# Attention probabilities transposed by DMA as 16-bit halves, with the heads of branches A and B at new slots

## The chip, the cores and the metric

The kernel runs on one core of a Trainium2 chip. The metric is the device time of one execution in microseconds. TensorE is called PE below, its weight loads PEld, VectorE DVE, ScalarE ACT, GpSimd POOL, and the queue that issues most DMAs SP. Each engine works through its own list of instructions strictly in the order in which the program issued them.

## The reference

One layer of a decoder, sequence 512, width 2048. The normed input is multiplied by one wide matrix that yields the inputs of three token mixers; two of them matter here, each with 12 heads of 64 channels:

```python
# branch A: window of 128 keys, in blocks of 128 queries by 256 keys
p = jnp.exp(scores - m)
denom = jnp.sum(p, axis=-1, keepdims=True) + jnp.exp(sink - m)
out = jnp.einsum('bnkgqs,bnskd->bnqkgd', p / denom, vb)
# branch B: causal attention with forget gates
sc = jnp.einsum('bqhd,bshd->bhqs', qb, k) * scale + cqb[..., None] - c[:, :, None, :]
p = jax.nn.softmax(jnp.where(mask[None, None], sc, NEG), axis=-1)
return jnp.einsum('bhqs,bshd->bqhd', p, v)
```

Branch C is a small cross attention. Each branch's output is gated, projected to 2048, weighted, summed, and goes through a last projection. All values are float32.

## The kernel before, in words

Every float32 product on PE is made of reduced-precision float32 products: an operand is split into a high part (`hi`, a cast on ACT) and a low part (`lo`, a subtraction on DVE), and hi·hi, hi·lo and lo·hi are summed in PSUM.

The program is one long stream of such products (`Stream`, L226). A unit of the stream multiplies 256 rows of a weight matrix with the activations: 24 matmuls of 384 or 512 columns. When unit i begins, the weights of unit i+1 are split (`w_split`, L206: two casts on ACT at L212, two subtractions on DVE at L215, the latter issued a little later) and those of unit i+2 are fetched (`weights`, L191, on SP). The split weights have two buffers, so the casts can't start before unit i-1 is done.

The attention heads are woven into that stream by a clock: `tick` (L146) is called after every third matmul of the stream and adds 0.5. Work is put on an agenda for a clock value (`later`, L143) or stands in a `Chain` (L165), a list of steps with offsets from a base. So one unit of 24 matmuls is 4 of the clock, and the place of a step in every engine's list is set by two tables: the base of a head (`BASES_B`, `BASES_A`) and the offset of a step (`STEPS_B`, `STEPS_A`). Preparations for pairs of heads (`prep`, `prep_q`, `prep_k`: transposes of queries or keys on PE, then two or four scalings on ACT through `q_stack` and `k_stack`) have slots of their own.

Branch B has its heads 0 to 5 beside the products that make the second half of B's queries, keys and values, and 6 to 11 beside A's. Branch A's 12 heads run beside the products z, mem and qC. One head of B (`head_B`, L583) does this: `s1(i)`, for query blocks i = 0 to 3: score products on PE of 128 to 512 keys, a fused add and row minimum on DVE (L600), an exponential on ACT (L603), a reciprocal and scaling (`scaled`, L579; on DVE for B, on POOL for A). POOL makes the biases (`sb`, L609). Then `s2(g)` transposes the probabilities in blocks of 128x128 on PE (L625) into PSUM, and `split` (L555) casts them to hi on ACT (L556) and subtracts lo on DVE (L558). Last `s3`: eight matmuls with V (L635, tile `avB`), each pair taking hi first and lo second, and `pv_out`, which adds up the two halves of the result. A head of B has 10 blocks to transpose; a head of A (`head_A`, L652; L688, L691, L702) has 7.

At the end of a product its four PSUM banks are read out on ACT (L437 for queries and keys, followed by squares for the norms at L404). In the stage of `mem` the activations, too, are split on ACT (`mhl`, L895). In a late stage the kernel already transposes by DMA for a part of its output (`flip_dma`: L1465 makes the halves, L1469 sends them, L1478 joins them).

Of the kernel before, what the change touches and what calls it, by code (L numbers as in the profile page):

```python
# [12 lines left out]
F32 = mybir.dt.float32  # L13
# [21 lines left out]
BASES_B = ((14, 24, 35.5, 46, 52, 70.5), (15, 24, 34.5, 47, 58, 72.5))  # L35
BASES_A = (12.5, 17, 23.5, 37.5, 43, 48.5, 52, 70.5, 75.0, 79.5, 81, 89)
BASES_C = (12.0, 19.5, 28.0, 33.5)
STEPS_B = (-12, -8.5, -2, -1.5, 0, 1, 1.0, 1.5, 3.5, 5, 12, 11.5, 14, 15.5)
STEPS_A = (-5.0, -1.0, -0.5, -1.5, 6.5, 8, 11, -6.5)
STEPS_C = (-8, -3.5, 0.5, 1, 8.0, 4.5, 10)  # L40

PREP_Q = ((-1.5, 22.0, 38.5), (2.5, 18.5, 45.5))
PREP_K = ((6.5, 28.0, 44), (7, 26.5, 53.5))
PREP_A = (6, 18.5, 39.0, 46, 66.0, 76.5)
PREP_KA = (6.0, 32.5, 47.5, 68.0)
# [12 lines left out]
def tile_hybrid_block(ctx, tc, xT, x, memT, mem, ng, mng, w_in, b_forget, gqa, gka, sinks, gqb, gkb, gqc, gkc,  # L58
# [100 lines left out]
    free = {"T": 2, "P": 2, "PT": 1, "Q": 3, "KH": 3, "KL": 2, "bias": 2, "cb": 2}  # L159
# [230 lines left out]

    def qk_tile(name, tag, n, bufs):
        return tokp.tile([P, NT, n], F32, tag=tag, bufs=bufs, name=name)
# [30 lines left out]
    def evac_qk(key, tag, n, hd, bufs, scale=rstd, nt=NT, after=None):  # L423
# [4 lines left out]
        def f(b, pb, c0=0):  # L428
            if after is not None:
                after(b, pb)  # L430
            if b == 0:
                state["t"] = tokp.tile([P, nt, n], F32, tag=tag, bufs=bufs, name=f"t_{key}")
# [10 lines left out]
    def evac_v(key, nh):  # L443
        state = {}

        def f(b, pb, c0=0):
            if b == 0:
                state["v"] = tokp.tile([P, NT, nh, P], F32R, tag="V", bufs=1, name=f"V_{key}")
# [3 lines left out]
            ac.activation(v[:, b, :, 0:64], src, AF.Copy, scale=rstd[:, b:b + 1])  # L452
            ve.scalar_tensor_tensor(out=v[:, b, :, 64:128], in0=src, scalar=rstd[:, b:b + 1],
                                    in1=f32(v[:, b, :, 0:64]), op0=ALU.mult, op1=ALU.subtract)
# [128 lines left out]
    def head_B(h, kv):  # L583
# [3 lines left out]
        def s1(i):  # L587
# [16 lines left out]
            later(DIV_B, lambda: scaled(pi, den, i, ve))  # L604

# [8 lines left out]
        def s2(g):  # L614
            p = s["p"]
            if g == 0:
                s["hi"] = at.p.tile([P, 1280], F32R, tag="PH", bufs=1, name=f"phB{h}")
                s["lo"] = at.p.tile([P, 1280], F32R, tag="PL", bufs=1, name=f"plB{h}")
            off = (0, 128, 384, 768)
            grp, o, n = (((0,), 0, 512), ((1, 3), 512, 512), ((2,), 1024, 256))[g]  # L620
            tb = tbank(f"ptB{h}_{grp[0]}")
            c = 0
            for j in grp:
                for i in range(j, NT):
                    pe.transpose(tb[:, c:c + P], p[:, off[i] + j * P:off[i] + (j + 1) * P], ident)  # L625
                    c += P
            split(s["hi"][:, o:o + n], s["lo"][:, o:o + n], tb[:, :n])

        def s3():
            q, kh, kl, v, hv, cb = kv()  # L630
            av = avbank(f"avB{h}")
            for j in range(NT):
                n = S - j * P
                for w, t in enumerate((s["hi"], s["lo"])):
                    pe.matmul(av[:, j * P:], v[:, j, hv, :], t[:, BOFF[j]:BOFF[j] + n],  # L635
# [3 lines left out]
        def done():  # L639
# [5 lines left out]
                 (o[8], [], lambda: s1(2)), (o[9], [], lambda: (s1(3), done())),  # L645
                 (o[10], ["T", "PT"], lambda: s2(0)), (o[11], ["T"], lambda: s2(1)),
                 (o[12], ["T"], lambda: (s2(2), release("P"))), (o[13], ["T"], lambda: (s3(), release("PT")))]
# [4 lines left out]
    def head_A(h, kv):  # L652
# [27 lines left out]
        def s2(g):  # L680
            pv = s["p"]
            if g == 0:
                s["hi"] = at.p.tile([P, 1280], F32R, tag="PH", bufs=1, name=f"phA{h}")
                s["lo"] = at.p.tile([P, 1280], F32R, tag="PL", bufs=1, name=f"plA{h}")
            tb = tbank(f"ptA{h}_{g}")
            c = 0
            for j in (2 * g, 2 * g + 1):
                pe.transpose(tb[:, c:c + P], pv[:, j, 128:256], ident)  # L688
                c += P
                if j < NT - 1:  # L690
# [216 lines left out]
    def evac_m(b, pb):  # L907
# [10 lines left out]
        if t == 1:  # L918
            toks["mv"] = (v[:, 0], v[:, 1])
# [695 lines left out]
```

## Time and profile before

| | |
|---|---|
| median of 3 runs | 1481.18 us (1481.14 to 1482.17) |
| span of the profiled execution | 1480.7 us, 20354 instructions; the page gives no other time of it |
| PE busy | 1473.2 us, 99% |
| ACT busy | 727.5 us, 49% |
| heads of B, first half and second half | about 125 to 238 us and 250 to 360 us |
| heads of A | about 391 to 556 us |

The page is read from the top: busy time by engine, then the span in 40 slices, then the chain of work that ended last. PE is busy in every slice, so what keeps it busy or makes it wait sets the time; the other engines' idle time costs nothing unless PE waits for them.

### The profile page before, as it was taken

Reading aid. Unit: us, or ns where it says so; the run is one execution under the profiler, and the core shown is the slowest. Engines: PE = TensorE matmul, PEld = TensorE weight load, DVE = VectorE, ACT = ScalarE, POOL = GpSimd, SP = SyncE. Lnnn points to the kernel's source line nnn. Section 1 sums busy time; section 2 is a strip of 40 time slices with the busy share of each in tenths; the row PEclk is TensorE's granted clock in tenths of the full one; section 3 lists DMA queues with packets and bytes.
Section 4 is the critical chain, followed back from the end, with each engine's and each line's share of the span. In section 5 each row is a group of like instructions: output and inputs, shape, how many; then the busy total and the mean of one; then the engine's idle time right before and its main releaser. Section 6 shows DMA issues by size and latency. Waiting matters only on the chain.

```text
span 1480.7 us, 20354 instructions
## 1 busy us (share of the span) xinstructions
PE 1473.2 (99%) x7193; PEld 1272.6 (86%) x7193; DVE 1092.5 (74%) x1886; ACT 727.5 (49%) x1212; POOL 185.3 (13%) x223
## 2 busy tenths in 40 slices
PE   9999999999999999999999999999999999999998
PEld 9999999998888888888888888888888888888887
DVE  6385875775678666578888888888887566589997
ACT  5545654664467664555444443435354344245442
POOL 0121430331324430000000000000000201110000
PEclk9999999999999999999999999999999999999999
DMA  8774235333444323476667676767676876676674
GB/s 290 222 213 130 76 93 164 84 113 111 130 137 151 92 79 108 149 261 231 207 213 224 214 241 206 241 211 230 201 236 213 279 222 205 220 246 223 243 286 153
DMA packets 135630, 279.50 MB, mean 189 GB/s; under 512 B 22492, under 2 KB 62044, under 8 KB 135528
## 3 DMA queue, kind: packets, MB, share of 16 engines
q1 hardware_dynamic: 130488, 261.68, 55.8%
q10 hardware_dynamic: 5040, 16.53, 3.3%
q8 instruction: 56, 0.92, 0.2%
q14 instruction: 46, 0.38, 0.1%
HBM read 244.58 MB, written 31.48 MB: 186 GB/s over the span
## 4 chain that ended last, share of the span: by engine, by line
PE 96%; ACT 1%; DVE 1%; DMA 1%; issue 0%; POOL 0%; DVEq 0%; ACTq 0%; POOLq 0%
PE P L1085 41%; PE z L301 11%; PE qA L301 5%; PE kB L301 5%; PE vB L301 5%; PE uB L1085 4%; PE uA L1085 4%; PE qB L301 4%; PE qC L301 3%; PE kvA L301 3%; PE uC L1085 3%; PE mem L301 1%; PE avB L635 1%; PE ptB L625 1%; PE avA L702 1%; PE sB L577 1%
## 5 line engine op out<-in xcount | busy, mean ns | idle before, releaser
L215 DVE TENSOR_TENSOR wc<-wa,wb 128x512 fp32r<-128x512 f32 (+2 forms) x252 | 148.8, 629 | 75.3 <-ACT wb L212 71.7
L212 ACT CAST wb<-wa 128x512 fp32r<-128x512 f32 (+2 forms) x252 | 130.5, 567 | 146.3 <-PE z L301 34.5
L1127 ACT CAST wa<-rawl 128x1024 fp32r<-128x1024 f32 x85 | 89.4, 1052 | 208.1 <-DVE rawl L1017 149.8
L1017 DVE TENSOR_TENSOR rawl<-rawl 128x512 f32<-128x512 f32 x256 | 176.9, 692 | 6.3 <-DMA rawl<-in_w_out_dram 1.9
L1130 DVE TENSOR_TENSOR wc<-rawl,wa 128x1024 fp32r<-128x1024 f32 x85 | 105.0, 1235 | 52.0 <-ACT wa L1127 50.3
L1130 DVE TENSOR_TENSOR we<-rawl,wd 128x512 fp32r<-128x512 f32 (+1 forms) x128 | 122.2, 954 | 4.5 <-ACT wd L1127 0.9
L1401 POOL TENSOR_TENSOR y<-y,gA 128x512 f32<-128x512 f32 x16 | 28.1, 1788 | 727.8 <-DVE gA L1399 727.8
L1127 ACT CAST wd<-rawl 128x512 fp32r<-128x512 f32 (+1 forms) x128 | 106.9, 835 | 23.8 <-DVE rawl L1017 20.1
L301 PE MATMUL z<-ah,wb 128*128 128x512 f32 x256 | 101.8, 398 | 0.0
L301 PE MATMUL z<-ah,wc 128*128 128x512 f32 x256 | 99.9, 390 | 0.0
L301 PE MATMUL z<-al,wb 128*128 128x512 f32 x256 | 99.8, 390 | 0.0
L1127 ACT CAST wb<-rawl 128x1024 fp32r<-128x1024 f32 x43 | 45.3, 1053 | 87.4 <-DVE rawl L1017 62.1
L1085 PE MATMUL P<-wd,xhx 128*128 128x512 f32 x192 | 74.8, 390 | 0.0
L1085 PE MATMUL P<-we,xhx 128*128 128x512 f32 x192 | 74.7, 389 | 0.0
L1085 PE MATMUL P<-wd,xlx 128*128 128x512 f32 x192 | 74.7, 389 | 0.0
L1130 DVE TENSOR_TENSOR wb<-rawl,wb 128x1024 fp32r<-128x1024 f32 x43 | 52.5, 1222 | 25.5 <-ACT wb L1127 25.3
L1014 DVE TENSOR_TENSOR R<-P,R 128x512 f32<-128x512 f32 (+1 forms) x90 | 57.1, 674 | 6.4 <-PE P L1085 5.8
L301 PEld LDWEIGHTS z<-ah,wc 128*128 128x128 f32 x256 | 48.0, 188 | 10.2
L301 PEld LDWEIGHTS z<-ah,wb 128*128 128x128 f32 x256 | 48.1, 188 | 9.3 <-DVE zA L939 0.3
L301 PEld LDWEIGHTS z<-al,wb 128*128 128x128 f32 x256 | 48.2, 188 | 9.0
L581 POOL TENSOR_SCALAR pA<-pA,denA 128x256 f32<-128x256 f32 (+1 forms) x48 | 45.0, 953 | 79.5 <-DVE denA L580 79.5
L1085 PE MATMUL P<-wa,xlx 128*128 128x512 f32 x128 | 49.8, 389 | 0.0
(410 smaller groups left out, 4184.8 us busy)
## 6 DMA issues: line engine op xcount, KB each, us to landing
rawl<-in_w_in_dram SPq DMA_DIRECT2D x144, 512.0 KB, 4.5
rawl<-in_w_out_dram SPq DMA_DIRECT2D x48, 512.0 KB, 4.8
wa<-in_w_in_dram SPq DMA_DIRECT2D x62, 384.0 KB, 3.5
wa<-in_w_in_dram SPq DMA_DIRECT2D x64, 256.0 KB, 3.1
rawl<-in_w_in_dram SPq DMA_DIRECT2D x48, 256.0 KB, 4.1
gates<-R ACTq DMA_DIRECT2D x24, 512.0 KB, 7.3
wa<-in_w_in_dram SPq DMA_DIRECT2D x16, 512.0 KB, 3.7
wa<-in_w_mem_dram SPq DMA_DIRECT2D x16, 512.0 KB, 3.7
```

Of the source, the lines that this page charges most:

```text
L212: ac.copy(hi[:, :n], raw[:, i, :n])
L215: ve.tensor_sub(lo[:, :n], raw[:, i, :n], f32(hi[:, :n]))
L301: pe.matmul(pb, a, m, start=b in fresh, stop=last and not todo[b])
L577: pe.matmul(dst, q[:, qs], kl[:, ks], start=False, stop=True)
L581: engine.tensor_scalar(p, p, den[:, 4 + i:5 + i], None, op0=ALU.mult)
L625: pe.transpose(tb[:, c:c + P], p[:, off[i] + j * P:off[i] + (j + 1) * P], ident)
L1014: ve.tensor_tensor(out, a, b, op=ALU.add)
L1017: ve.tensor_tensor(out, a, b, op=ALU.subtract)
L1085: pe.matmul(*args, **kw)
L1127: ac.copy(hi[:, :k, :], src)
L1130: return lambda: ve.tensor_tensor(lo[:, :k, :], src, f32(hi[:, :k, :]), op=ALU.subtract)
L1401: po.tensor_tensor(y, y, g, op=ALU.add)
```

## The change

The 204 transposes of probabilities on PE go away (12 heads of B with 10, 12 of A with 7). In their place, for every head:

- `halves`: POOL copies the float32 probabilities, seen as pairs of 16-bit numbers, into a tile in which all first halves and all second halves lie apart (2560 numbers per partition for B in five copies, 1792 for A in three);
- `send`: one DMA transpose on SP, of 20 blocks of 128x128 16-bit numbers for B and 14 for A;
- `join`: one copy on ACT that puts the halves together again, into float32 in SBUF;
- `s2`: one cast on ACT to hi (1280 or 896 columns), and `s2l`: one subtraction on DVE to lo. Before there were three casts and three subtractions per head of B and two and two of A, each read from PSUM.

`head_A` gets the same functions with 896 columns; its `halves(True)` copies the first two query blocks, `halves(False)` the other two.

The new tiles take places freed by cutting V of branch B in two pieces (heads 0 to 3 and 4 to 5 of a half) and by reusing others. New names in `free` (S1, S2, RW) keep heads from overtaking each other there. All heads' bases, the preparations' slots and the offsets change.

```diff
-BASES_B = ((14, 24, 35.5, 46, 52, 70.5), (15, 24, 34.5, 47, 58, 72.5))
+BASES_B = ((14, 26, 38, 46, 58, 70), (14, 26, 38, 46, 58, 70))
-STEPS_B = (-12, -8.5, -2, -1.5, 0, 1, 1.0, 1.5, 3.5, 5, 12, 11.5, 14, 15.5)
+STEPS_B = (-12, -8.5, -2, -1.5, 0, 1, 1.0, 1.5, 3.5, 5, 10.5, 16.5, 18, 19, 20.5, 4.5)
-STEPS_A = (-5.0, -1.0, -0.5, -1.5, 6.5, 8, 11, -6.5)
+STEPS_A = (-5.0, -1.0, -0.5, -1.5, 6.5, 10.5, 11.5, -6.5, 3, 3.5, 12.5, 13.5)
...
+    def spare(n, name, dtype=F32, cols=1280):
+
+        return tokp.tile([P, 1280 * 4 // mybir.dt.size(dtype)], dtype, tag=f"X{n}", bufs=1, name=name)[:, :cols]
...
@@ evac_v
-            ac.activation(v[:, b, :, 0:64], src, AF.Copy, scale=rstd[:, b:b + 1])
+            for t, hs in zip(v, (slice(0, 4), slice(4, 6))):
+                ac.activation(t[:, b, :, 0:64], src[:, hs, :], AF.Copy, scale=rstd[:, b:b + 1])
...
@@ head_B
+            s["p", i] = pi
+            if i > 1:
+                later(DIV_B + 0.5, lambda: halves(i))
...
-            for j in grp:
-                for i in range(j, NT):
-                    pe.transpose(tb[:, c:c + P], p[:, off[i] + j * P:off[i] + (j + 1) * P], ident)
-                    c += P
-            split(s["hi"][:, o:o + n], s["lo"][:, o:o + n], tb[:, :n])
+        def halves(i):
+
+            if i == 0:
+                s["s1"] = spare(0, f"s1B{h}", U16, 2560).rearrange("p (e j n) -> p e j n", e=2, n=P)
+            src = u16(s["p", i]).rearrange("p (j n e) -> p e j n", n=P, e=2)
+            n = min(i + 1, 3)
+            po.tensor_copy(s["s1"][:, :, i:i + 3 * n - 2:3, :], src[:, :, :n, :])
+            if i == 3:
+                po.tensor_copy(s["s1"][:, :, 7:8, :], src[:, :, 3:4, :])
+                release("P")
+
+        def send():
+            s["s2"] = spare(1, f"s2B{h}", U16, 2560)
+            sy.dma_start_transpose(out=s["s2"].rearrange("p (x n) -> p x n", n=P),
+                                   in_=s["s1"].rearrange("p e j n -> p (e j n)"))
+            release("S1")
+
+        def join():
+            s["t"] = spare(2, f"ptB{h}")
+            ac.copy(u16(s["t"]).rearrange("p (n e) -> p e n", e=2), s["s2"].rearrange("p (e n) -> p e n", e=2))
+            release("S2")
+
+        def s2():
+            s["hi"] = at.p.tile([P, 1280], F32R, tag="PH", bufs=1, name=f"phB{h}")
+            s["lo"] = at.p.tile([P, 1280], F32R, tag="PL", bufs=1, name=f"plB{h}")
+            ac.copy(s["hi"], s["t"])
+
+        def s2l():
+            ve.tensor_tensor(s["lo"], s["t"], f32(s["hi"]), op=ALU.subtract)
+            release("RW")
...
-                 (o[10], ["T", "PT"], lambda: s2(0)), (o[11], ["T"], lambda: s2(1)),
-                 (o[12], ["T"], lambda: (s2(2), release("P"))), (o[13], ["T"], lambda: (s3(), release("PT")))]
+                 (o[10], ["S2"], send), (o[11], ["RW"], join), (o[12], ["PT"], s2), (o[13], [], s2l),
+                 (o[14], ["T"], lambda: (s3(), release("PT")))]
...
@@ head_A
-                (o[4], ["T", "PT"], lambda: s2(0)), (o[5], ["T"], lambda: (s2(1), release("P"))),
-                (o[6], ["T"], lambda: (s3(), release("PT")))]
+                (o[8], ["S1"], lambda: halves(True)), (o[9], [], lambda: halves(False)), (o[4], ["S2"], send),
+                (o[5], ["RW"], join), (o[6], ["PT"], s2), (o[10], [], s2l), (o[11], ["T"], lambda: (s3(), release("PT")))]
```

The tables move instructions on every engine; three places show how. The line numbers of the changed program are its own. First, ACT's list before, around head 1 of the first half of branch B: its three casts to `phB`, with the exponentials of the next head (`pB`, `denB`), the weight casts (`wb`, each x2 belongs to one unit), and the next pair's queries (`qB`).

```order
L556 CAST phB_1748<-ptB_0_1750 128x512
L556 CAST phB_1748<-ptB_1_1756 128x512
L212 CAST wb_1762<-wa_1694 128x384 x2
L603 ACTIVATE pB_1773,denB_1774<-pB_1773,denB_1774 128x128
L404 ACTIVATE sq_qB_1804<-t_qB_1625 128x384
L556 CAST phB_1748<-ptB_2_1806 128x256
L603 ACTIVATE pB_1773,denB_1774<-pB_1773,denB_1774 128x256
L212 CAST wb_1848<-wa_1766 128x384 x2
L566 COPY avsB_1859<-avB_1832 64x512
```

ACT's list now, for the same head: the copy from `s2B` to `ptB` is the join, and the cast to `phB` is `s2`.

```order
L212 CAST wb_1822<-wa_1754 128x384 x2
L616 ACTIVATE pB_1783,denB_1784<-pB_1783,denB_1784 128x384
L649 COPY ptB_1855<-s2B_1759 128x2x1280
L551 ACTIVATE qB_1878<-tqB_1873,gs_qb 64x512
L551 ACTIVATE qB_1880<-tqB_1873,gs_qb 64x512
L616 ACTIVATE pB_1783,denB_1784<-pB_1783,denB_1784 128x512
L655 CAST phB_1886<-ptB_1855 128x1280
L212 CAST wb_1894<-wa_1826 128x384 x2
L579 COPY avsB_1963<-avB_1938 64x512
```

The casts to hi were spread over three places, each behind its own transposes; now the join and one long cast stand between the last two exponentials of the next head and the weight casts of a unit, with the next pair's queries between them.

Second, DVE's list at the same place, before: the first two subtractions of `plB` of head 1, with the weight subtractions (`wc`), norms (`nr_qB`, `t_qB`) and the next head's first score block.

```order
L215 TENSOR_TENSOR wc_1691<-wa_1615,wb_1690 128x384 x2
L570 TENSOR_TENSOR ysB_1657<-avB_1648,avsB_1671 64x512
L415 TENSOR_TENSOR t_qB_1625<-t_qB_1625,nr_qB_1627 128x384
L558 TENSOR_TENSOR plB_1749<-ptB_0_1750,phB_1748 128x512
L558 TENSOR_TENSOR plB_1749<-ptB_1_1756,phB_1748 128x512
L600 ISA pB_1773,denB_1774<-sB_0_1775,biB_0_1723 128x128
```

DVE's list now: one subtraction of `plB`.

```order
L552 SCALAR_TENSOR_TENSOR qB_1878<-tqB_1873,gs_qb,qB_1878 64x512
L552 SCALAR_TENSOR_TENSOR qB_1880<-tqB_1873,gs_qb,qB_1880 64x512
L215 TENSOR_TENSOR wc_1895<-wa_1826,wb_1894 128x384 x2
L658 TENSOR_TENSOR plB_1887<-ptB_1855,phB_1886 128x1280
L593 RECIPROCAL denB_1784<-denB_1784 128x1
L594 TENSOR_SCALAR pB_1783<-pB_1783,denB_1784 128x512
```

`plB` now stands behind the subtractions `wc` that read the weights cast after `phB`, and ahead of the scaling of the next head's last block.

Third, ACT's list in the stage of `mem`, for head 3 of branch A, before (the casts to `phA` are its splits):

```order
L556 CAST phA_4926<-ptA_0_4928 128x512
L212 CAST wb_4934<-wa_4889 128x512 x2
L895 ACTIVATE mhl_4940<-mraw_4938,mngt 128x256 x2
L556 CAST phA_4926<-ptA_1_4958 128x384
L538 ACTIVATE qA_4981<-tqA_4976,gs_qa 64x512
```

and now:

```order
L212 CAST wb_4857<-wa_4839 128x512 x2
L739 COPY ptA_4870<-s2A_4797 128x2x896
L950 ACTIVATE mhl_4863<-mraw_4861,mngt 128x256 x2
L745 CAST phA_4893<-ptA_4870 128x896
L212 CAST wb_4901<-wa_4864 128x512 x2
L579 COPY avsA_4931<-avA_4919 64x512
```

The join comes right behind one unit's weight casts, and the cast to hi right ahead of the next unit's.

104 lines of the change are left out of this document (59 added, 45 removed).

## The prediction

> **What bounds the kernel now.** I read the page's head first, then what PE waited for, then the two attention stages (the first window is six heads of B, the second the twelve of A; columns: window, busy us and count of PE, PEld, DVE, ACT, POOL, then clock, DMA share, GB/s).
>
> ```profile
> span 1480.7 us, 20354 instructions
> ...
> PE 1473.2 (99%) x7193; PEld 1272.6 (86%) x7193; DVE 1092.5 (74%) x1886; ACT 727.5 (49%) x1212; POOL 185.3 (13%) x223
> ```
> ```profile
> PE warm_up L1540 <- DVE wz L1537: 1.9, 1, 1.9
> PE ptA L688 <- DVE kl L550: 0.7, 1, 0.7
> PE kB L301 <- ACT t_qB L437: 0.2, 1, 0.2
> ```
> ```profile
> 252.00:360.00 108.00, 108.00 (x610) 100.10 (x609) 77.34 (x203) 60.87 (x138) 33.96 (x52) 1.00 0.39 119
> 391.00:556.00 165.00, 164.22 (x867) 138.07 (x866) 116.60 (x310) 106.31 (x245) 63.06 (x67) 1.00 0.38 116
> ```
>
> PE is the bound everywhere, at full granted clock, and once started it waited 0.9 us in all. So what leaves PE is gained in full, and each new wait of PE is lost in full: no later stage has slack to give it back. ACT is at 56% beside B and 64% beside A: it has room on average, but a list in order can be late at one place all the same.
>
> **What leaves PE.** The price of a transpose is how far it pushes the next matmuls, for the busy figures overlap. PE's timeline around head 0 of B (a group of 8 and one of 2) and head 0 of A (one of 4):
>
> ```profile
> 139.30 0.34 PE L301 MATMUL qB<-wb,al 128*128 128x384 f32 x1
> 139.48 1.04 PE L625 MATMUL ptB<-ident,pB 128*128 128x128 f32 x8
> 140.53 0.34 PE L301 MATMUL qB<-wc,ah 128*128 128x384 f32 x1
> ...
> 142.62 0.34 PE L301 MATMUL qB<-wb,al 128*128 128x384 f32 x1
> 142.79 0.38 PE L625 MATMUL ptB<-ident,pB 128*128 128x128 f32 x2
> 143.19 0.34 PE L301 MATMUL qB<-wc,ah 128*128 128x384 f32 x1
> ```
> ```profile
> 398.95 0.39 PE L301 MATMUL z<-ah,wc 128*128 128x512 f32 x1
> 399.85 0.39 PE L301 MATMUL z<-al,wb 128*128 128x512 f32 x1
> ...
> 401.46 0.39 PE L301 MATMUL z<-ah,wc 128*128 128x512 f32 x1
> 402.36 0.39 PE L301 MATMUL z<-al,wb 128*128 128x512 f32 x1
> ```
> ```profile
> 224.32 10.45 PE vB L301 x60
> ...
> 359.25 10.96 PE kvA L301 x48
> ```
>
> The last rows (of the chain) give the pitch: 10.45/60 = 0.174 us for 384 columns, 10.96/48 = 0.228 for 512. From the matmul before a group to the second one behind it would be two pitches. The 8 cost 1.23 - 0.35 = 0.88 us, the 2 cost 0.57 - 0.35 = 0.22, the 4 and the 3 of A 0.90 - 0.46 = 0.44 each. Twelve heads each: 12 x 1.10 + 12 x 0.88 = **23.8 us gained**.
>
> **What comes on ACT.** Join is a copy of 2560 16-bit numbers for B, 1792 for A, written with a stride of two. The kernel has the same form, and one that reads with a stride:
>
> ```profile
> L1478 ACT COPY y3s<-yh 128x512 uint16<-128x512 uint16 x8 | 5.6, 764 | 3.3 <-DMA y_alpha<-y3s 3.3
> L1465 ACT COPY gC<-y 128x1024 uint16<-128x1024 uint16 x8 | 8.0, 1043 | 20.6 <-DVE y L1014 20.6
> ...
> L1127 ACT CAST wa<-rawl 128x1024 fp32r<-128x1024 f32 x85 | 89.4, 1052 | 208.1 <-DVE rawl L1017 149.8 <-PE P L1085 46.8 <-PE uA L1085 5.8
> L212 ACT CAST wb<-wa 128x512 fp32r<-128x512 f32 x128 | 73.0, 619 | 79.3 <-PE z L301 34.5 <-PE kvA L301 14.2 <-issue 7.7
> L212 ACT CAST wb<-wa 128x384 fp32r<-128x384 f32 x108 | 50.0, 511 | 52.1 <-PE vB L301 25.1 <-PE qB L301 11.0 <-issue 5.7
> ```
>
> All the extra time of the writing form as a fixed cost would make join 2.3 to 2.7 us (1043/1024 x 2560 = 2.6 and below); all of it per number, 764/512 x 2560 = 3.8. I take **3.0 for B and 2.1 for A**, for L1478 is the same form, less a part that is fixed. The Trainium skill (ScalarE: Activation LUTs, What ACT_TABLE_LOAD costs) says about 186 ns plus 0.833 ns per element, whatever the type; for 1024 that agrees with the 1043 ns of L1465, for 512 it says 613 where L1478 has 764. By it join would be near 2.3 us, and the time forecast below some 14 us lower.
> The cast to hi of 1280 columns is 1.3 us by L1127, of 896 0.9: about what the three, or two, before it took. So each head of B gives ACT 3 us more, of A 2: on average ACT would still fit (60.9 + 18 in a window of 108 us). The place decides.
>
> **The wait that this makes, head by head.** Head 1 of B, in the order of ACT that the section on the change shows: exponential, join, two query scalings, exponential, cast to hi, two weight casts; then DVE: two weight subtractions, lo; then PE's second `avB` matmul, which needs lo. The other durations, and how PE and ACT lie to each other now (scores of 384 keys at 161.10, their exponential at 162.74):
>
> ```profile
> 161.10 0.33 PE L576 MATMUL sB<-kB,qB 128*128 128x384 f32 x1
> ...
> 163.47 0.60 PE L531 MATMUL tqB<-ident,t_qB 128*128 128x128 f32 x4
> 163.82 0.42 PE L301 MATMUL kB<-wb,ah 128*128 128x384 f32 x1
> ```
> ```profile
> 162.74 0.62 ACT L603 ACTIVATE pB<-pB,denB 128x384 f32<-128x384 f32 x1
> 163.26 0.19 ACT L603 ACTIVATION_READ_ACCUMULATOR pB<-pB,denB 128x1 f32 x1
> 164.11 1.38 ACT L538 ACTIVATE qB<-tqB,gs_qb 64x512 fp32r<-64x512 f32 x2 [0.66 <-PE tqB L531]
> 165.75 0.72 ACT L603 ACTIVATE pB<-pB,denB 128x512 f32<-128x512 f32 x1 [0.26 <-DVE denB L600]
> ```
> ```profile
> L1130 DVE TENSOR_TENSOR wc<-rawl,wa 128x1024 fp32r<-128x1024 f32 x85 | 105.0, 1235 | 52.0 <-ACT wa L1127 50.3 <-PE z L301 1.4
> ...
> L215 DVE TENSOR_TENSOR wc<-wa,wb 128x512 fp32r<-128x512 f32 x128 | 83.6, 690 | 36.6 <-ACT wb L212 36.5
> L215 DVE TENSOR_TENSOR wc<-wa,wb 128x384 fp32r<-128x384 f32 x108 | 56.7, 566 | 17.0 <-ACT wb L212 16.8
> ```
>
> From the start of the 384-key scores: the exponential begins after 1.6 us and takes 0.7, join ends at 5.3, queries (1.4) at 6.7, exponential (0.8) at 7.5, hi at 8.8, weight casts (0.9 the pair) at 9.7; on DVE the second weight subtraction ends at 10.3 and lo (1280/1024 x 1.235 = 1.5) at 11.8. In that time PE has, in the new order, the scores themselves (0.35), 30 matmuls of 384 (5.2), the 512-key scores (0.46), four transposes of queries (0.44) and small scores (0.15): it wants lo at 6.6 + 0.2 = 6.8. **PE waits 5.0 us.** Nothing hides it; the order of ACT and DVE is fixed, so a DMA that lands early doesn't help.
> The other heads of B go the same way, by what ACT's list has between join and the casts: heads 4 and 10 the bare list, 4.1 and (beside 512-column matmuls, which give PE more to do) 2.8; heads 1 and 7 a pair of queries, 5.0 and 5.4; 3 and 9 the reading out of banks and squares, 5.4 and 4.6; 0 and 6 that and four key scalings, 8.0 and 7.4; 2 and 8 have the key scalings ahead of join, 3.8 each; 5 and 11 nothing, 1.5 and 0. **Sum 51.8 us**, minus or plus 9 for join at 2.3 or 3.8.
> A, head 3, from the start of a unit of mem: two weight casts, join, two `mhl` splits, hi, the first cast of the next unit, on DVE its subtraction and lo:
>
> ```profile
> L895 ACT ACTIVATE mhl<-mraw,mngt 128x256 fp32r<-128x256 f32 x16 | 7.4, 502 | 0.4 <-DMA mraw<-in_memT_dram 0.4
> ```
>
> 1.1 + 2.1 + 0.9 + 0.9 + 0.6 + 0.6 + 1.1 = 7.3 against 4.9 of PE's work before lo is wanted (21 matmuls of 512): 2.3 us. Heads 1 to 4 lie there: 2.2, 3.5 (with queries and four exponentials), 2.3, 3.1; head 0 1.8; heads 5 to 11, beside longer units, 4.1 in all. **Sum 17.0 us**, minus or plus 6.
> Free of cost: V in two pieces (four more short copies on ACT and on DVE per half), the new bases as such (the last head of C ends at the same value of the clock), and DVE's subtractions (one long for three).
>
> **POOL and the DMA.** Neither is in the sum, by these rows (landing times are of 16 blocks; B sends 20, A 14):
>
> ```profile
> L1469 SPq DMA_TRANSPOSE yh<-gC x4: 1637/2816/3939, 1191.7 to 1238.0; - x4
> ...
> DMA to landing us min/median/max: 3.8/4.9/6.0
> ```
> ```profile
> L581 POOL TENSOR_SCALAR pA<-pA,denA 128x256 f32<-128x256 f32 x36 | 34.4, 970 | 0.0
> ...
> L609 POOL TENSOR_SCALAR biB<-cb,cq 128x512 f32<-128x512 f32 x12 | 10.7, 891 | 2.9 <-DVE denB L600 2.4 <-DVE denB L580 0.5
> ```
>
> For B the DMA has 6 of the clock, 36 matmuls or 6.3 us plus the attention's own, against 4.8 to 7.5 us: mostly hidden, since join also waits for an exponential. For A, POOL scales (four times, 3.9 us), copies 1792 numbers (3.1 us by L609, 6.8 by L581), then the DMA takes 3.3 to 5.3: 10.3 to 16.0 us, against 7 of the clock from scaling to join, 42 matmuls or 9.6 us and about 11.5 with the attention's own, and 1 more that join waits for weight casts anyhow. At L609's price it fits, and POOL's plainest row is the nearest to a copy.
>
> **The rivals.**
> 1. ACT runs ahead of PE: its list reaches join early enough that hi and lo are there when `avB` and `avA` come, and only the gain is left: 1480.7 - 23.8 + 0.5 = **1457 us**. It decides at a mean wait of 23.8/24 = 1.0 us per head; below that the change wins. For it: ACT's share stays under 80%. Against it: the exponential ahead of join can't run before its scores, and from there the bare list of head 4 takes 4.1 us too long; even with join at nothing 1.1 us would be left.
> 2. POOL copies at L581's price and A's joins come 1 to 3 us late on top: half of that, 20 us, gives **1546**.
> 3. The crossbar is the bound: B's 20 blocks always land after the longest time, 7.5 us, up to 1.2 us behind the 36 matmuls, and push join back by that: 12 x 1.2 = 14 us, **1540**. It decides where the landing passes the exponential ahead of join. The Trainium skill (VectorE: DVE Perf Modes, Rules for kernel authors) speaks for it and against the change: transposes of 128x128 go to TensorE where PSUM will do. Its 1309 ns for one through the crossbar would make 26 us of 20; the trace's 3.8 to 6.0 us for 16 disagree.
>
> **How the numbers follow.** 1480.7 - 23.8 + 51.8 + 17.0 = 1525.7 of span; the median of the runs lies 0.5 above the span, so **1526 us**. Chances: this forecast 0.70, rival 2 0.10, rival 3 0.05, rival 1 0.12, and 0.03 that waits and gain cancel to within 0.2%, which is about what a measurement of this kernel can tell from no change. Both bounds of join give 1511 and 1541; I have walked some heads only roughly, so the range goes from **1496** (half of A's waits and a third of B's gone) to **1556** (rival 2 with the dear join). Faster 0.12, same 0.03, slower 0.85.
>
> **What would show it.** In the changed profile PE's waits should be led by `avB <- DVE plB` and `avA <- DVE plA`, some 4 us and 1.5 us a head, with DVE idle before `wc` for ACT's `wb`; join near 3.0 and 2.1 us. PE's count falls by 204 transposes. It is wrong if `avB` waits under 1 us a head, if join waits for the DMA (ACT idle, released by it), or if PE waits at the stream's own matmuls for late weights from SP.

## The result, and the profile after

The changed kernel takes **1577.0 us** (median of 4, 1575.4 to 1581.0) against 1481.6 for the kernel before beside it: a ratio of 1.065, 95% interval 1.063 to 1.066. It is slower, as forecast, but by 95 us where the forecast had 45, and above the upper end of the range.

The page's head after, with PE's row and the clock's row of the 40 slices (the profiled execution took 1581.0 us, the longest of the four):

```profile
span 1579.2 us, 20058 instructions
...
PE 1499.9 (95%) x6989; PEld 1282.7 (81%) x6989; DVE 1101.5 (70%) x1858; ACT 786.1 (50%) x1208; POOL 244.6 (15%) x319
...
PE   9998878888998799899999999999999999999998
...
PEclk9999889989998899999999999999999999999999
```

The same two rows before:

```profile
PE   9999999999999999999999999999999999999998
...
PEclk9999999999999999999999999999999999999999
```

PE has the 204 transposes fewer, yet it is busy 27 us longer. The clock's row points to why: it held nines from end to end before, and now shows eights, all in the slices of attention where PE's row falls below nine. PE's waits (us in all, times, longest):

```profile
PE avB L667 <- DVE plB L658: 24.5, 11, 2.8
PE avA L757 <- DVE plA L748: 15.7, 10, 3.7
PE avB L667 <- ACT phB L655: 8.6, 6, 2.7
PE avA L757 <- ACT phA L745: 8.5, 7, 3.3
PE kB L301 <- ACT t_qB L446: 3.1, 2, 2.5
PE qA L301 <- ACT t_qA L446: 3.1, 2, 2.5
```

The first four rows are the waits that were forecast, in the places that were forecast; the last two, for the readout of banks, stand at places that were not. All PE idle time between its first and last matmul is 72.7 us (1.3 before). What the clock does beside them is seen in consecutive stretches of 3.41 us, the second head of B in its middle (window, busy us of PE, PEld, DVE, ACT, POOL, then the clock):

```profile
172.05:175.46 3.41, 3.29 (x20) 2.97 (x18) 0.59 (x4) 3.37 (x3) 2.60 (x6) 1.00 0.26 94
175.46:178.88 3.42, 0.49 (x1) 0.19 (x1) 1.99 (x4) 3.29 (x6) 0.00 (x0) 1.00 0.00 0
178.88:182.29 3.41, 1.42 (x4) 1.33 (x5) 2.80 (x7) 0.50 (x2) 0.81 (x2) 0.50 0.42 115
182.29:185.70 3.41, 3.41 (x15) 3.41 (x14) 0.80 (x4) 1.12 (x3) 1.69 (x5) 0.50 0.66 151
185.70:189.12 3.42, 3.42 (x21) 3.42 (x20) 2.08 (x6) 1.27 (x4) 1.27 (x3) 1.00 0.60 187
...
213.01:216.42 3.41, 1.90 (x11) 1.58 (x10) 0.55 (x1) 3.41 (x7) 1.54 (x3) 1.00 0.00 0
216.42:219.84 3.42, 0.93 (x4) 0.29 (x2) 1.88 (x4) 2.52 (x6) 1.33 (x1) 1.00 0.00 0
219.84:223.25 3.41, 2.64 (x9) 2.54 (x10) 2.62 (x6) 0.42 (x1) 2.03 (x3) 0.50 0.45 120
```

A stretch in which PE stood still for most of the time is followed by one at half clock; the half clock stays while stretches hold waits and goes after a busy one (15 matmuls in 182.29, 21 in the next). The idle 1.51 us of 213.01 changed nothing. The trace holds 16 such drops before the last instructions, all 3.41, 6.83 or 10.24 us long. PE's busy time inside them is 79.5 us, so about half of it, **39.7 us**, is what the clock cost. That is an upper bound: the pitch of matmuls of 384 columns is 0.320 us at half clock for 0.174, that of 512 columns 0.427 for 0.227, so that 46 to 47% of the time, some 37 us, was lost. The forecast has no such term.

The sum by measured parts: 1480.7 - 21.3 (transposes, measured alone below) + 71.4 (idle time) + 39.7 (clock) = 1570.5. Of the 8.7 left to 1579.2 (some 11 with 37 us for the clock), part is how PE starts again after a wait:

```profile
213.15 0.34 PE L301 MATMUL vB<-wb,al 128*128 128x384 f32 x1
215.00 0.44 PE L301 MATMUL vB<-wb,ah 128*128 128x384 f32 x1 [1.51 <-ACT t_kB L446]
215.28 0.34 PE L301 MATMUL vB<-wc,ah 128*128 128x384 f32 x1
215.46 0.34 PE L301 MATMUL vB<-wb,al 128*128 128x384 f32 x1
```

The first matmul behind a wait takes 0.28 us to the next one where the pitch is 0.175; with some 50 waits that is about 5 us, counted as busy. The rest, 4 to 6 us, stays open.

### The profile page after: what moved, and what is told of

It reads as the page before. It is cut to its first block, busy times and chain, and to the rows that moved or that the text cites. A ratio compares the mean times of both kernels' runs of the same rounds, so it can differ in the third digit from the quotient of the medians.

```text
span 1579.2 us, 20058 instructions
## 1 busy us (share of the span) xinstructions
PE 1499.9 (95%) x6989; PEld 1282.7 (81%) x6989; DVE 1101.5 (70%) x1858; ACT 786.1 (50%) x1208; POOL 244.6 (15%) x319
## 4 chain that ended last, share of the span: by engine, by line
PE 59%; DMA 2%; ACT 2%; DVE 1%; issue 1%; POOL 1%; ACTq 0%; DVEq 0%; POOLq 0%; SPq 0%
PE P L1140 38%; PE z L301 8%; PE uA L1140 4%; PE uB L1140 3%; PE uC L1140 3%; PE qC L301 1%; DMA s2A<-s1A 1%; POOL pA L594 1%; DMA gates<-R 1%; DMA gB<-gates 0%; PE avA L757 0%; PE avC L810 0%; ACT wb L212 0%; ACT ptA L739 0%; DMA wa<-in_w_mem_dram 0%
## 5 line engine op out<-in xcount | busy, mean ns | idle before, releaser
L215 DVE TENSOR_TENSOR wc<-wa,wb 128x512 fp32r<-128x512 f32 (+2 forms) x252 | 152.1, 641 | 134.8 <-ACT wb L212 126.6
L1456 POOL TENSOR_TENSOR y<-y,gA 128x512 f32<-128x512 f32 x16 | 28.1, 1792 | 733.8 <-DVE gA L1454 733.8
L616 ACT ACTIVATE pB<-pB,denB 128x128 f32<-128x128 f32 (+3 forms) x48 | 27.0, 562 | 57.0 <-DVE denB L613 56.9
```

The source lines that it names most:

```text
L215: ve.tensor_sub(lo[:, :n], raw[:, i, :n], f32(hi[:, :n]))
L616: later(EXP_B, lambda: ac.activation(pi, pi, AF.Exp, bias=nm, scale=-1.0, accum_out=den[:, i:i + 1]))
L1456: po.tensor_tensor(y, y, g, op=ALU.add)
```

## Experiments

Theory Q: PE waits because the join stands in ACT's list ahead of other work, and the clock falls after the waits. Each experiment starts from the changed kernel, unless it says otherwise. "Idle" is PE's idle time between its first and last matmul, "clock" half of its busy time at half clock, both from the trace of one execution. The expectations count both more widely: idle as the span less PE's busy time (79 us for the changed kernel in place of 72.7), the clock as half of all time at half clock, idle or not (47 in place of 39.7). `e2_filler`, `e3_av_later`, `e4_no_dma_wait`, `e8_wait_long` and `e9_wait_short` are one execution each, the others the median of four (`e19_no_transposes_new_slots` of ten).

**Is it the clock?** `e2_filler` fills the wait with matmuls whose result is overwritten:

```diff
             av = avbank(f"avB{h}")
+            for _ in range(14):
+                pe.matmul(av, ah[0][:, 0, :P], al[0][:, 0, :], start=True, stop=True)
...
             av = avbank(f"avA{h}")
+            for _ in range(9):
+                pe.matmul(av, ah[0][:, 0, :P], al[0][:, 0, :], start=True, stop=True)
```

> The changed kernel with products that nothing reads put in front of the attention's products with V: 14 matmuls of 512 columns for each head of B, 9 for each of A, into the same bank, overwritten afterwards. They add 12 x 23 x 0.228 = 63 us of TensorE work and stand where it waited. Theory Q: the waits of 72.7 us shrink to some 20 (those for banks, and the longest heads), the clock stays at full (0.99 or more), and the time FALLS although work is added: 1457 + 63 + 20 = 1540 us. Rival C (the clock drops for another reason that the change brings, such as the DMA transposes): the clock stays near 0.97 and the time is 1577 or more.

Measured: 1569.5 us, idle 30.9, clock 10.2. 276 matmuls more, and 7.5 us less than the changed kernel. Not 1540: the filler, 0.23 us a matmul, is longer than many of the waits that it fills. But 63 us of work were added and only 41.8 us of idle time taken off; by the waits alone the time would have risen by 21 us. The clock's part fell by 29.5, which makes up for it.

`e8_wait_long` and `e9_wait_short` put waits into the kernel before, whose attention has no crossbar (the diff is of the long one; the short one has one copy of 64 columns):

```diff
             av = avbank(f"avB{h}")
+            pe.matmul(av, s["hi"][:, :P], s["hi"][:, :512], start=True, stop=True)
+            for _ in range(2):
+                ac.copy(av[:, :512], av[:, :512])
```

> The kernel before, no crossbar in it, with a wait put in ahead of each of the 24 products with V in A and B: one more matmul of 512 columns into the product's bank, two ScalarE copies of the whole bank onto itself (0.6 us each), and only then the product, which overwrites the bank. The added matmuls are 24 times 0.23 us, 5 us. TensorE then waits about 1.6 us for the two copies and up to 1.5 us for what stands ahead of them in ScalarE's list, 1.6 to 3 us each time, 50 us in sum. Theory H (the clock is halved for 3.41 us wherever TensorE stood still for more than half of a stretch of 3.41 us, as all traces so far show): about two in three of these waits halve it, at 1.7 us each, 25 us more, so 1555 to 1570 us and a mean clock of 0.98. Rival N (waits of under 3.4 us don't touch the clock; in the changed kernel it fell for another reason, the crossbar's transfers or the like): the clock stays at 1.0 and the time is 1530 to 1540 us.

> The same added wait made short: one ScalarE copy of 64 columns (0.25 us) in place of two of 512. TensorE waits 0.6 us at least and up to 1.5 us more where ScalarE's list is behind. Theory H: waits under 1.7 us don't halve the clock, so it falls at most six times, at 1.7 us each, and the time is 1481 plus 5 us of matmuls plus 25 to 30 us of waits plus at most 10: 1510 to 1525 us. Rival N: the same without the 10. If the clock falls after waits of 1 us too, theory H has its threshold wrong.

Measured: 1547.0 us (idle 44.1, clock 12.0) and 1517.2 us (idle 20.8, clock 6.3). The long one falls between both forecasts: its waits were shorter than I had put them. Of its 24 waits at the products the 17 of 1.26 to 1.69 us left the clock alone, the four of 3.5 to 3.7 us halved it each time, and of three of 2.1 to 2.3 us one did. Two of its places, the first with a wait of 3.55 us, the second with one of 1.26:

```profile
144.55:147.96 3.41, 1.36 (x9) 0.96 (x7) 1.18 (x4) 3.37 (x7) 0.00 (x0) 1.00 0.42 120
147.96:151.37 3.41, 1.91 (x6) 1.72 (x7) 2.08 (x4) 1.39 (x3) 0.00 (x0) 0.50 0.00 0
151.37:154.79 3.42, 3.42 (x13) 3.42 (x13) 0.27 (x2) 1.59 (x4) 0.00 (x0) 0.50 0.00 0
```
```profile
223.05:226.47 3.42, 2.16 (x13) 1.78 (x12) 3.35 (x11) 1.69 (x6) 2.66 (x5) 1.00 0.15 44
226.47:229.88 3.41, 3.41 (x20) 3.24 (x21) 0.26 (x2) 1.13 (x3) 0.18 (x1) 1.00 0.69 225
```

In the short one no wait is over 2.96 us, and the clock still fell three times, each time behind a stretch that holds most of one of its four waits of 2.5 to 3.0 us. Rival N (waits under 3.4 us don't touch the clock, the crossbar lowers it) falls; and the four DMA transposes that the kernel before makes from 1191.7 to 1238.0 us left its clock at full. The threshold comes from all 20 traces: every change of the clock lies on a grid of 3.413 us, to 3 ns, and for each cell of it between PE's first and last matmul its idle time stands here against the clock of the next.

| idle in a cell at full clock | cells | next cell at half clock |
|---|---|---|
| under 1.5 us | 8515 | 0 |
| 1.5 to 1.8 us | 38 | 11 |
| 1.8 to 2.0 us | 19 | 17 |
| 2.0 us and more | 98 | 98 |

From a cell at half clock, 51 of 52 with 0.5 us idle or more were followed by another, and 3 of 128 with less.

**Is it the crossbar?** `e4_no_dma_wait` joins the probabilities themselves (`w` is their 16-bit view), so that nothing waits for the transfer:

```diff
-            ac.copy(u16(s["t"]).rearrange("p (n e) -> p e n", e=2), s["s2"].rearrange("p (e n) -> p e n", e=2))
+            ac.copy(u16(s["t"]).rearrange("p (n e) -> p e n", e=2), s["w"].rearrange("p (n e) -> p e n", e=2))
```

> The changed kernel, but the join reads the untransposed probabilities instead of what the DMA brought, so nothing waits for the halves on GpSimd or for the DMA transpose (both are still issued); the probabilities are not transposed here. Theory Q: the DMA landed in time nearly always, so 1577 us less at most 8. Rival D (halves or crossbar too late): most of the loss goes, under 1530 us.

Measured: 1574.1 us, idle 71.5. The transfer's landing is worth 3 us at most, less than the changed kernel's executions differ by; rival D falls.

**Is it the place in the lists?** Three edits of `STEPS_B` and `STEPS_A` alone. `e3_av_later` moves the product with V (1.5 and 2.5 later), `e12_early_b` moves B's join, high half and subtraction (2 to 2.5 earlier), `e10_early_join` does both, and a little of the same in A:

```diff
-STEPS_B = (-12, -8.5, -2, -1.5, 0, 1, 1.0, 1.5, 3.5, 5, 10.5, 16.5, 18, 19, 20.5, 4.5)
-STEPS_A = (-5.0, -1.0, -0.5, -1.5, 6.5, 10.5, 11.5, -6.5, 3, 3.5, 12.5, 13.5)
+STEPS_B = (-12, -8.5, -2, -1.5, 0, 1, 1.0, 1.5, 3.5, 5, 10.5, 14.5, 15.5, 16.5, 22, 4.5)
+STEPS_A = (-5.0, -1.0, -0.5, -1.5, 6.5, 10, 10.5, -6.5, 3, 3.5, 11.5, 16)
```

> The changed kernel with one number of each step table changed: the products with V 1.5 of the clock later for B (9 matmuls, 1.6 us) and 2.5 later for A (15 matmuls, 3.4 us). Theory Q: waits fall from 72.7 us by 12 x 1.6 for B and nearly all of A's 24, to about 30; the half clock falls in the same measure, from 92 us of it to about 40; time near 1457 + 30 + 20 = 1507 us. With waits alone, and a clock that has nothing to do with them: 1577 - 43 = 1534 us.

> Only B's three slots of the early join (join 2, high half 2.5, subtraction 2.5 earlier); the products with V and all of A as in the changed kernel. Theory L: the 33 us that TensorE waits for B's two parts fall under 10, the 8 us for the first preparations' readouts under 4, and of the 47 us that the clock costs those that lie in B's stages, about 30, fall under 10; A's are as they were: 1522 us (1510 to 1535). Rival J: the waits of B move to the readouts, and the time is above 1555 us. Rival D: above 1560 us, with ScalarE waiting for the transfers.

> The changed kernel with its join left on ScalarE, and only the slots moved: in B the join 2, the high half 2.5 and the subtraction 2.5 earlier, the product with V 1.5 later; in A the join 0.5, the high half 1 and the subtraction 1 earlier, the product 2.5 later. No copy on GpSimd runs beside VectorE that didn't before. Theory L (the wait is made by the places in ScalarE's and VectorE's lists: the join lands behind key scalings and projections' readouts, the high half behind the next ones, the subtraction behind a pair of weight subtractions that itself waits for ScalarE; the price of the join hardly matters): TensorE waits for the two parts under 8 us in sum, TensorE's idle time falls from 79 to about 35 us, the clock costs under 15 us, and the time is 1495 us (1478 to 1508). Rival J (the join's 3.1 and 2.2 us of ScalarE are what is missing, wherever they stand): the wait only moves to the projections' readouts and the weights, idle time stays above 50 us and the time above 1520 us. Rival D (the transfer lands too late for an early join, so that ScalarE stands still for it): ScalarE waits over 1 us a head for the transfer, and the time is above 1530 us.

Measured: `e3_av_later` 1534.3 us (idle 47.3, clock 20.1), `e12_early_b` 1538.7 (48.5, 19.5), `e10_early_join` 1520.8 (37.5, 13.6). In `e12_early_b` the waits of `avB` go from 33.1 to 9.0 us:

```profile
PE avB L667 <- DVE plB L658: 5.1, 5, 1.0
PE avB L667 <- ACT phB L655: 3.9, 3, 2.1
```

Three slots take 38 us off, half of it clock. `e3_av_later` came out at the 1534 us that its expectation gives for waits alone, but not by that way: idle time fell by 25 us where that sum has 43, and the clock's part by 20 where it has none. Theory L (the place decides) holds for the waits of the product. The times stayed 17 to 27 us above the forecasts: PE's waits for the readouts of the projections stayed, and in `e10_early_join` a new wait came up in A: `mem` for its weights, 13.5 us for 3.0 in the changed kernel. SP's queue stands at A's transposing transfers (line L734), the weight loads come behind them, and ACT waits for those:

```profile
SPq L734 <- POOL biA L689: 42.1, 7, 9.2
SPq L734 <- POOL s1A L728: 16.9, 4, 7.2
```
```profile
ACT wb L212 <- DMA wa<-in_w_mem_dram: 15.6, 5, 5.5
```

`e13_send_later_a` sends these transfers 3 later (in `STEPS_A` 9.5 for 6.5, then 13, 13.5, 14.5 and 18.5):

> The kernel with the early join, and A's transposing transfer sent 3 later, its join and high half 3, its subtraction 3 and its product with V 2.5 later. In the early-join kernel SyncE's queue stands at A's transfers until GpSimd has scaled and copied the halves (42 and 17 us in sum), the loads of the weights behind them are issued up to 8 us late, ScalarE waits 15.6 us for five of them, and TensorE 13.5 us for their casts and remainders. Theory S (that is what is left in A): SyncE's wait at A's transfers falls under 25 us, ScalarE's for those weights under 5, TensorE's idle time from 44 to about 33 us, the clock's cost from 17 to about 11, and the time is 1504 us (1496 to 1512). Rival F (the weights are late because ScalarE and VectorE are full there, not for the queue): the time stays within 5 us of 1520.8, and TensorE's waits for the memory projections stay above 10 us.

Measured: 1512.7 us (idle 35.8, clock 6.8). ACT's wait for these weights falls to 6.5 us, PE's waits for `mem` from 13.5 to 8.7; SP still stands 64 us at the transfers (80 before). So rival F falls, and theory S is only half borne out: the late weights cost less, but the time is 8 us shorter where it gave 16, and SP's 59 us until POOL's work was done fell to 35, not under 25.

**The join on another engine.**

```diff
-            ac.copy(u16(s["t"]).rearrange("p (n e) -> p e n", e=2), s["s2"].rearrange("p (e n) -> p e n", e=2))
+            po.tensor_copy(u16(s["t"]).rearrange("p (n e) -> p e n", e=2), s["s2"].rearrange("p (e n) -> p e n", e=2))
```

`e5_join_pool` has this in A and B, `e6_pool_av_later` with later products.

> The changed kernel with one edit: the copy that joins the 16-bit halves back into 32-bit probabilities runs on GpSimd (2.6 us for B and 1.8 us for A by the rate of its own 16-bit copies, 0.83 ns an element and 0.2 us) in place of ScalarE (3.1 and 2.2 us); every slot stays. Theory Q (TensorE waits because the join stands in ScalarE's list ahead of the bank readouts and of the high halves, and the clock falls after these waits): ScalarE's list is 3.1 us a B head and 2.2 us an A head shorter, the join starts as soon as its transfer has landed, TensorE's idle time falls from 79 us to under 35 us, the time lost to the clock from 47 us to under 15 us, and the time is 1490 us (1470 to 1510). Rival P (GpSimd is the wrong engine: writing every second 16-bit element takes it twice its rate, 4.5 us, or its list is held up by the wait for the transfer, so that the biases come late): 1530 us or more. Rival V (VectorE's subtraction, not ScalarE's list, is what is late): idle time stays above 60 us and the time above 1555 us.

> The join on GpSimd, and three slots moved: the product with V 1.5 (B) and 2.5 (A) later, the subtraction that makes the low part 0.5 earlier in both. Theory Q: nearly all waits for the two parts are gone, the clock falls at most three times, and the time is the changed kernel's own work without waits, about 1454 us, and 10 to 15 us of the waits that the slots of the preparation bring: 1467 us (1458 to 1480), which is below the 1481 us of the kernel before. Rival P (GpSimd's join comes late): above 1500 us. Rival W (the waits move to the weights' subtractions and the readouts of the projections, as some did when the product was moved alone): 1485 to 1500 us.

Measured: 1589.8 us (idle 83.4, clock 39.4), slower than on ACT, and 1531.5 (47.1, 15.9), hardly better than the later products alone. Both against the theory. The first head of `e5_join_pool`, POOL's row and DVE's two beside it:

```profile
142.04 3.42 POOL L649 COPY ptB<-s2B 128x2560 uint16<-128x2560 uint16 x1
```
```profile
141.95 3.87 DVE L215 TENSOR_TENSOR wc<-wa,wb 128x384 fp32r<-128x384 f32 x2 [0.69 <-ACT wb L212]
145.74 0.55 DVE L613 CUSTOM_DVE_ANT_0 pB<-sB,biB 128x384 f32<-128x384 f32 x1
```

This pair of subtractions takes 1.23 us in the changed kernel and 3.87 here: it ends 0.4 us behind the copy, and DVE's add for the next scores comes late. Another, at 208.47, takes 3.61 us beside a copy and 1.24 in the changed kernel. The Trainium skill (SBUF — State Buffer, section SBUF: two separate sides) says that a GpSimd operation that reads SBUF and a VectorE operation with two SBUF inputs exclude each other for a whole instruction; this trace agrees, with 3.87 us. And although the join ended at 145.5, 3 us earlier than before, the high half ran only at 151.8, for it kept its place in ACT's list behind key scalings and exponentials: in this head the place of the high half, and not the price of the join, set the wait.

`e14_join_dve_b` puts B's join on DVE on top of `e13_send_later_a`, `e20_join_dve_later` the same 1 later, `e15_join_dve_both` A's, too (product with V at 20.5 and 18, A's join 0.5 earlier):

> The same with B's join on VectorE in place of ScalarE. No run here shows such a copy on VectorE; between its 1.2 ns an element for 32-bit copies of 512 and ScalarE's 1.21 ns it would be about 3 us. Theory B (in B the join's 3.1 us of ScalarE stand ahead of the projections' bank readouts, which TensorE waits for 11 us): these waits fall under 4 us, VectorE, which has 70 us idle in B, takes the join at the cost of 3 to 5 us of late remainders, and the time is 6 to 12 us below the kernel with A's later transfer. Rival G (VectorE takes more than 3.5 us, or GpSimd's copies stop it as they did when the join was on GpSimd): the time is at least as long as that kernel's, with TensorE waiting for scores or for weights' remainders.

> The kernel with B's join on VectorE (1504 us), with that join, the high half and the subtraction 1 later. VectorE stood 8.8 us still for four transfers that had not landed, and weights' remainders behind it came late to TensorE by 7.6 us in four places. If that is the cause, these waits fall by 4 to 6 us and the clock's cost by 2: 1497 us (1493 to 1501). If not, the product with V waits for its parts again or the time stays: 1502 us or more.

> The join on VectorE in A as well as in B (it took 1.63 us for 2560 there; 1792 should take 1.2), the early slots, the product with V at B's own old slot (20.5) and in A at 18. Theory L: with 2.2 us less of ScalarE a head the memory projections' casts come in time, TensorE's idle time falls from 35 to about 28 us, the clock's cost from 13 to about 7: 1492 us (1485 to 1500). Rival G (VectorE is now too full in A, the weights' remainders are late): 1504 us or more.

Measured: **1504.0 us** (ratio 1.015, 1.013 to 1.016; idle 29.0, clock 11.9), 1505.2 and 1507.3. On DVE the join costs half of what it does on ACT or POOL:

```profile
L649 DVE COPY ptB<-s2B x12: 1592/1626/1652, 140.4 to 363.4; 128x2560 uint16<-128x2560 uint16 x12
```

Theory B holds: 8.7 us off, and PE's waits for the readouts go from 11.0 to 4.2 us, at the cost of later remainders (PE's waits for `wc` at the products beside B go from 1.0 to 8.3 us). The other two gained nothing on it, so neither DVE's standing still for transfers nor ACT's joins in A were shown to be what is left.

**The slots and the transposes, each alone.** `e1_slots_only` is the kernel before with the new `BASES` and `PREP` tables; `e18_no_transposes` the kernel before without the 204 transposes, its parts split straight from the probabilities (shown for B, A's lines go likewise); `e19_no_transposes_new_slots` both:

```diff
-                    pe.transpose(tb[:, c:c + P], p[:, off[i] + j * P:off[i] + (j + 1) * P], ident)
-            split(s["hi"][:, o:o + n], s["lo"][:, o:o + n], tb[:, :n])
+            split(s["hi"][:, o:o + n], s["lo"][:, o:o + n], p[:, o:o + n])
```

> The kernel before (transposes on TensorE, its own step offsets) with the six tables of bases and preparations of the changed kernel. Theory Q (ScalarE's and VectorE's lists make TensorE wait for the low part; every wait then costs a second time, because the granted clock drops to half for 3.4 us or more behind it): the slots as such are free, 1481 us give or take 6, clock 0.99 or more. Rival S (the new slots themselves jam the lists): a large part of the 96 us is here already, over 1520 us.

> The kernel before with the 204 transposes of A's and B's probabilities left out and nothing in their place: the halves are split straight from the untransposed probabilities, so the two parts hold other numbers. Slots, banks and the rest are the kernel before's. This prices the first term of the forecast, 23.8 us for the transposes, by itself. Theory M (that term was too large: in the twelve crossbar kernels TensorE's busy time without what the half clock adds is 1457 to 1462 us, 13 below the kernel before's 1473): 1468 to 1472 us, TensorE busy 1460. Rival O (the forecast's 23.8 us were right, and something in the crossbar kernels makes TensorE's other work 10 us longer): 1457 to 1460 us, TensorE busy 1449.

> The same at the changed kernel's slots for heads and preparations. The kernel before took 20 us more at these slots, 14 of them waits and 3 clock. If the slots cost the same without the transposes: 1487 to 1491 us, and hardly any of what is left in the best crossbar kernel (1504) could be its way through the crossbar beyond 15 us. If they cost less where no transposes stand in TensorE's list: 1470 to 1480 us.

Measured: `e1_slots_only` 1501.9 us (idle 14.9, clock 3.3), 20 above the kernel before, which neither side of its expectation had. `e18_no_transposes` 1465.9 (ratio 0.989, 0.988 to 0.991):

```profile
span 1464.0 us, 19941 instructions
...
PE 1451.9 (99%) x6989; PEld 1251.8 (86%) x6989; DVE 1095.1 (75%) x1886; ACT 726.1 (50%) x1212; POOL 193.4 (13%) x223
```

PE's busy time falls by 21.3 us (1473.2 - 1451.9), so theory M falls and the forecast's term was nearly right; the time falls by 15.6 (the profiled span by 16.7), since 4.7 us of small waits come up. The changed kernel's PE is busy 48.0 us longer than this one, with the same 6989 matmuls: 37 to 40 us are the clock, about 5 the restarts, and what is left of rival O's 10 us stays open. `e19_no_transposes_new_slots` 1485.6 (1482.3 to 1488.2): the slots cost 20 us without transposes as with them.

`e17_old_slots_b` and `e16_old_slots` give `e15_join_dve_both` the old slots of heads and preparations, in B and in both (B's heads are shown):

```diff
-BASES_B = ((14, 26, 38, 46, 58, 70), (14, 26, 38, 46, 58, 70))
+BASES_B = ((14, 24, 35.5, 46, 52, 70.5), (15, 24, 34.5, 47, 58, 72.5))
```

> The same with B's heads and B's preparations back at the slots of the kernel before. Theory T (part of what is left is the new slots themselves, which cost the kernel before 20 us when it was given them alone): the waits for the readouts and remainders at the preparations in B fall by 8 us and the clock's cost by 3: 11 us below the kernel with VectorE's joins, about 1481. Rival U (the new slots are needed by the longer way through the crossbar: at 6 to 11.5 us between heads the product with V waits again): 5 us or more above it.

> The same with A's heads and preparations, too, at the slots of the kernel before, where two pairs of A heads stand 1.5 and 3.5 apart. Theory T: 5 to 10 us below the kernel with B's old slots, 1473 us, below the 1481 of the kernel before. Rival U: heads that share one buffer for the transposed probabilities push each other back, the product with V waits for its parts in A, and the time is above the kernel with B's old slots.

Measured: 1516.1 us (idle 40.3, clock 6.7) and 1521.9 (41.8, 13.1): slower by 9 and 15, rival U. With these offsets the way through the crossbar needs the wider slots; transposes that cost nothing at all save 15.6 us at the old slots, and the new slots cost 20. No version through the crossbar beats the kernel before; at the new slots transposes that cost nothing give 1485.6, still above it. Which slot makes the 20 us wasn't tried.

## Why the forecast was right, and where it was wrong

- **What bounds the kernel.** Right that a new wait of PE has no slack behind it. Wrong is "each new wait of PE is lost in full": it is lost in more than full. This is **the step that failed**. I noted the full granted clock and took it as given, though it fell behind every stretch of 3.413 us in which PE stood still for 2 us or more. The profiled span of 1579.2 is 53.5 us above the forecast's 1525.7; 37 to 40 us of clock and about 5 of restarts are 42 to 45 of them, 2.5 are the smaller gain from the transposes, 2.6 more idle time. The Trainium skill (TensorE: Matmul & The Clock Gate, Part 1) describes a gate that watches stretches of 3413 ns, halves the clock after one idle stretch, and advises against idle gaps over 3.4 us. The runs agree with the stretches of 3.413 us; they differ on the gap, for 2 us idle inside one stretch halved it in 98 of 98. By its rule one wait, the longest of 3.7 us, could have halved the clock in the changed kernel; it was halved 16 times.
- **What leaves PE:** 23.8 us forecast, 21.3 measured alone, so 12% too large. "Gained in full" is not quite so either: 4.7 of the 21.3 us went to new small waits.
- **Join:** 3.0 and 2.1 us forecast, 3.10 and 2.23 measured (L649, L739). Right: 0.2 us and 1.13 ns a number fit both.
- **B's waits:** 51.8 forecast; `avB` waited 33.1, and the readouts of four projections 8.5. Head 1, walked step by step, gave 5.0 against 5.04 measured; heads 2, 8 and 11 gave 3.8, 3.8 and 0 against 3.3, 3.3 and 0. The other heads were 0.3 to 2.1 us too large. Most so were 0 and 6 (8.0 and 7.4 against 5.2 each, 3.1 of it at the readouts): PE's waits at the readouts put it later against ACT's list, which I had not followed on.
- **A's waits:** 17.0 forecast, 24.1 measured at `avA`. Heads 0 to 4 are 14.3 against 12.9; heads 5 to 11, which I had walked only roughly, 9.8 against 4.1. All idle time grew by 71.4 us, against 68.8 in the sum. That this fits so well is luck: B's waits were put too high, A's too low, and some 6 us of other waits weren't in the sum at all.
- **POOL and DMA free:** right. A's transfers landed 3.5 us after their issue, B's 4.1, and joins waited 2.3 us for them in all. Late weights behind the transfers on SP's queue stood among the signs of being wrong, but not in the sum; that cost showed only when other waits had gone.
- **New bases free of cost:** wrong, in the kernel before they cost 20 us. In the version with DVE's joins the old ones are worse, so the step can't be added to the sum as it stands.
- **The range.** Its ends don't follow from what is said of them: half of A's waits and a third of B's gone would be 1500 us, rival 2 with the dear join 1561. The measured 1577.0 lies above either, for no term of the range touches the clock.
- **The rivals.** 1 fell: the mean wait was 57.2/24 = 2.4 us, above its point of 1.0. 2 fell:

```profile
L728 POOL COPY s1A<-pA 128x1024 uint16<-128x1024 uint16 x12 | 13.8, 1147 | 0.0
L726 POOL COPY s1A<-pA 128x512 uint16<-128x512 uint16 x12 | 9.1, 760 | 0.0
L724 POOL COPY s1A<-pA 128x256 uint16<-128x256 uint16 x12 | 5.4, 450 | 0.7 <-DMA s2A<-s1A 0.7
```

  A's copies take 2.4 us a head, not 6.8. 3 fell by the landing times and by `e4_no_dma_wait`.
- **What would show it:** `avB` and `avA` led PE's waits, at 2.8 and 2.0 us a head for "some 4 and 1.5".

## What to carry to other kernels

Where PE is busy throughout, a forecast of new waits needs a second term: for each stretch of 3.4 us, ask whether PE stands still for 1.8 us or more in it (115 of 117 such stretches halved the clock here), and if so add 1.5 to 1.7 us for the clock, and again for each stretch that then holds over 0.5 us of waits. In a kernel with one list per engine the place of an instruction can cost more than its length: three slots were worth 38 us, and moving the join to another engine at its old place cost 13. Before a step is taken off the bounding engine, try the kernel without that step: here that caps the gain at 15.6 us, less than the new slots cost.

## What the hardware showed that was not expected

- The granted clock is decided in a fixed grid of 3.413 us: never halved behind a cell with under 1.5 us idle (0 of 8515), always behind one with 2.0 or more (98 of 98).
- After a wait PE's first matmul takes some 0.1 us longer to the next (0.28 for 0.175 at 384 columns).
- A 16-bit copy of 2560 numbers that writes with a stride of two takes 3.10 us on ACT, 3.23 on POOL and 1.63 on DVE.
- A GpSimd copy stops a VectorE subtraction of two SBUF operands until it ends: 3.87 us for a pair that takes 1.23 without it.
